# A decoder layer on one core: the first stage takes its operands from a host-transposed copy of the input

## The chip, the core and the metric

The kernel runs on one NeuronCore of a Trainium2 chip. It computes one decoder layer for 1040 rows (16 meta tokens and 1024 tokens) of 1024 channels. The metric is the time on the device of one execution, in microseconds; less is better. The core has five engines that run side by side, each with its own instruction queue in a fixed order: TensorE (PE, matmuls into PSUM), VectorE (DVE), ScalarE (ACT), GpSimd (POOL), and SyncE (SP), which here issues the DMA transfers from HBM. An instruction that waits holds up everything behind it on its engine.

## The reference

The layer is an RMS norm, an input projection, a mix of differential attention (4 heads) and a gated linear recurrence (4 heads), an output projection, and a feed-forward block with a short convolution. The change touches only the norm and the first projections:

```python
def rmsnorm(x, g):
    xf = x.astype(jnp.float32)
    y = xf * lax.rsqrt(jnp.mean(xf * xf, axis=-1, keepdims=True) + EPS)
    return (y * g.astype(jnp.float32)).astype(x.dtype)

h = jnp.concatenate([meta, x], axis=1)          # 1040 rows
a = rmsnorm(h, ln_mix_pre[l])
proj = a @ w_in[l]                              # 1024 x 3584: dq, dk, dv, hq, hf, hi, hg
```

## The kernel before, in words

Every float32 operand of a projection is split into a high part, rounded to the type that PE multiplies at full rate, and a low part, the rest. A projection adds three products: high weight with high operand, low weight with high operand, high weight with low operand. The operand must have channels on the partitions: `ahi` and `alo` hold the normed input transposed, as 8 slices (k = 0 to 7) of 128 channels by 1040 rows.

The rows come in nine blocks (block 0 is the 16 meta rows, blocks 1 to 8 have 128 rows) and in three groups of three blocks: group 0 has 272 columns in the transposed operand, groups 1 and 2 have 384 each. The first stage makes `ahi` and `alo` for all groups and, between, computes dq, dk and dv of attention head 0. For one group and one of the three, that is 24 matmuls: 8 slices times 3 products. All further projections read the same `ahi` and `alo`; the next is `pi_hf`.

Before the change a block goes this way. `load_x` brings its rows. `pre_stat` squares and sums them on ACT and makes 1/rms (two more small ACT instructions). `pre_scale` multiplies the rows on DVE by that factor and by the gain, which is spread over the partitions in `gb` (made by two matmuls `pg` of a column of ones with the gain row). `pre_turn` transposes the 128x128 pieces on PE into PSUM (tile `px`). `pre_hi` casts from PSUM on ACT and `pre_lo` subtracts on DVE. For blocks 4 and 5 `far_block` scales on ACT and POOL.

The order on PE is the order of the program, written by hand (`manual_schedule`). On ACT, DVE and POOL a scheduler places the instructions, except where `state["ordered"]` is set: then they keep the order in which they are written. Before the change this holds for blocks 0 to 5 and group 0; groups 1 and 2 are interleaved by generators. `evac` functions of the attention head (`attn_in`) take a finished projection from PSUM: `ev_q` and `ev_k` write high parts on ACT and low parts (`q`, `kl`) on DVE, `ev_v` copies to `vt`, which `to_nat` (called by `flush`) turns on PE (tile `pn_va`) into `avn`.

Three side jobs lie in the same stretch. `smalls` loads small tables and makes `lb` from `lg`. `lam_terms` makes `nlam` from `lv` by way of `le`. `bias_tables` makes one table per head: it casts a one-hot table to `oh` on ACT, spreads the bias values into `tbb` on DVE, multiplies them on PE (`pb`), copies the result to `rb` on DVE and stores it. Most helpers issue through one wrapper, so the profile names line 58 for them; tiles tell them apart.

## Time and profile before

| | |
|---|---|
| median of 3 runs | 1275.96 us (1275.55 to 1276.72) |
| the profiled execution, first to last instruction | 1275.4 us |
| PE busy | 1256.7 us, 99% of the span |
| DVE, ACT, POOL busy | 913.9, 687.3, 507.2 us |
| mean granted clock of PE | 0.999 |
| HBM read, written | 134.24 MB, 52.17 MB |
| first projection matmul starts | 11.52 us |
| first matmul of pi_hf starts | 57.75 us |

A row of the timeline gives start and duration in us, the engine (PEld is PE's loading of weights, SPq the issue of a DMA), the source line, the operation, the tile written and those read, and how many instructions were merged into the row; in brackets is the idle time before it and what ended it. A row by groups gives after the count the busy time in us and the mean ns of one instruction, and behind the second bar the idle time before such instructions. A row by stretches gives the stretch, its length, the busy time of PE, PEld, DVE, ACT and POOL with counts, then the granted clock, the mean busy share of the DMA engines and the GB/s that they moved.

### The profile page before, as it was taken

The numbers are of one execution on the slowest core, as the hardware profiler recorded it, in microseconds if no ns is written. First come the engines' busy times: TensorE is split into PE (matmuls) and PEld (weight loads), VectorE is DVE, ScalarE is ACT, GpSimd is POOL, SyncE is SP. The second block draws the span as 40 slices with busy tenths as digits, with TensorE's granted clock in tenths as the row PEclk, the third lists the DMA queues.
The fourth block names the chain that finished last, engine by engine and source line by source line (L and its number), as shares of the span: only waits on it lengthen the run. The fifth ranks groups of instructions, "written<-read, shape, count | busy, mean of one in ns | idle before, by whom it ended". The sixth has DMA issues, their size and how long they took to land.

```text
span 1275.4 us, 26064 instructions
## 1 busy us (share of the span) xinstructions
PE 1256.7 (99%) x10166; PEld 1172.8 (92%) x10166; DVE 913.9 (72%) x1492; ACT 687.3 (54%) x1638; POOL 507.2 (40%) x390
## 2 busy tenths in 40 slices
PE   8999999999999999999999999999999999999997
PEld 6999999999999998778899999999999998878886
DVE  7565646565656564457899888898898877797586
ACT  8475456546654754356764544445535445564554
POOL 5232423241323311353067676676776731020121
PEclk9999999999999999999999999999999999999999
DMA  7336555373734533787322221322222247955363
GB/s 260 96 60 131 89 139 94 83 146 92 132 94 79 125 82 113 232 279 253 131 67 67 92 88 63 100 76 75 92 75 83 75 116 258 351 184 173 91 215 124
DMA packets 116705, 165.04 MB, mean 129 GB/s; under 512 B 10131, under 2 KB 57811, under 8 KB 116582
## 3 DMA queue, kind: packets, MB, share of 16 engines
q1 hardware_dynamic: 93350, 151.84, 37.1%
q0 software_dynamic: 23232, 11.54, 7.7%
q8 instruction: 80, 1.31, 0.4%
q14 instruction: 43, 0.35, 0.1%
HBM read 134.24 MB, written 52.17 MB: 146 GB/s over the span
## 4 chain that ended last, share of the span: by engine, by line
PE 46%; DVE 4%; ACT 2%; issue 1%; POOL 1%; DMA 0%; SPq 0%; DVEq 0%; ACTq 0%; POOLq 0%
PE pd L1586 5%; PE pd L1587 5%; PE pd L1585 5%; PE pb L1412 4%; PE pb L1411 4%; PE pb L1413 4%; PE pc L1412 3%; PE pc L1411 3%; PE pc L1413 3%; PE pa L1412 3%; PE pa L1411 3%; PE pa L1413 3%; DVE xh L58 1%; DVE t L58 1%; DVE c L58 1%
## 5 line engine op out<-in xcount | busy, mean ns | idle before, releaser
L1412 PE MATMUL pb<-t,uh 128*128 128x258 f32 x504 | 141.0, 280 | 0.8 <-DVE t L58 0.8
L1411 PE MATMUL pb<-t,uh 128*128 128x258 f32 x504 | 140.5, 279 | 0.8 <-DVE u L58 0.8
L1413 PE MATMUL pb<-t,ul 128*128 128x258 f32 x504 | 140.2, 278 | 0.0
L1586 PE MATMUL pd<-wl,gh 128*128 128x512 f32 (+1 forms) x312 | 121.0, 388 | 1.1 <-DVE wl L58 1.1
L1585 PE MATMUL pd<-wh,gh 128*128 128x512 f32 (+1 forms) x312 | 120.8, 387 | 0.5 <-DVE x L58 0.5
L1587 PE MATMUL pd<-wh,gl 128*128 128x512 f32 (+1 forms) x312 | 120.7, 387 | 0.0
L58 DVE SCALAR_TENSOR_TENSOR c<-uu,cwt,c 128x514 f32<-128x514 f32 (+1 forms) x88 | 106.9, 1214 | 0.0
L58 DVE SCALAR_TENSOR_TENSOR c<-ug,cwt,c 128x514 f32<-128x514 f32 (+1 forms) x88 | 101.4, 1153 | 0.0
L1412 PEld LDWEIGHTS pb<-t,uh 128*128 128x128 f32 x504 | 94.8, 188 | 1.0 <-DVE t L58 1.0
L1411 PEld LDWEIGHTS pb<-t,uh 128*128 128x128 f32 x504 | 94.8, 188 | 1.0 <-DVE u L58 1.0
L58 ACT ACTIVATE c<-c 128x514 f32<-128x514 f32 (+1 forms) x44 | 27.9, 634 | 125.5 <-DVE c L58 125.5
L1413 PEld LDWEIGHTS pb<-t,ul 128*128 128x128 f32 x504 | 94.8, 188 | 0.0
L1412 PE MATMUL pc<-t,uh 128*128 128x258 f32 (+1 forms) x336 | 93.9, 279 | 0.0
L1412 PE MATMUL pa<-t,uh 128*128 128x258 f32 (+1 forms) x336 | 93.9, 279 | 0.0
L1411 PE MATMUL pa<-t,uh 128*128 128x258 f32 (+1 forms) x336 | 93.6, 278 | 0.0
L1411 PE MATMUL pc<-t,uh 128*128 128x258 f32 (+1 forms) x336 | 93.6, 278 | 0.0
L1413 PE MATMUL pc<-t,ul 128*128 128x258 f32 (+1 forms) x336 | 93.4, 278 | 0.0
L1413 PE MATMUL pa<-t,ul 128*128 128x258 f32 (+1 forms) x336 | 93.4, 278 | 0.0
L58 POOL TENSOR_TENSOR ul<-ws,uh 128x512 fp32r<-128x512 f32 x42 | 69.2, 1647 | 59.6 <-ACT uh L58 59.6
L58 POOL TENSOR_TENSOR ws<-ra,ra 128x512 f32<-128x512 f32 x42 | 67.9, 1617 | 60.9 <-DMA ra<-in_wup_dram 34.1
L58 POOL TENSOR_TENSOR c<-c,c 128x514 f32<-128x514 f32 (+1 forms) x44 | 68.8, 1564 | 53.9 <-ACT c L58 50.5
L58 DVE TENSOR_TENSOR ul<-ra,uh 128x512 fp32r<-128x512 f32 x43 | 41.5, 966 | 46.6 <-POOL ul L58 46.6
(389 smaller groups left out, 4183.1 us busy)
## 6 DMA issues: line engine op xcount, KB each, us to landing
ra<-in_wup_dram SPq DMA_DIRECT2D x88, 256.0 KB, 2.6
mp<-msc SPq DMA_DIRECT2D x23, 512.0 KB, 5.7
tsc<-in_wdown_dram SPq DMA_DIRECT2D x44, 256.0 KB, 5.2
wi<-tsc SPq DMA_DIRECT2D x44, 256.0 KB, 3.0
gi<-gsc SPq DMA_DIRECT2D x33, 256.0 KB, 4.2
wi<-in_wdown_dram SPq DMA_DIRECT2D x33, 256.0 KB, 5.2
gsc<-c SPq DMA_DIRECT2D x22, 257.0 KB, 2.1
tsc<-in_wdown_dram POOLq DMA_DIRECT2D x22, 256.0 KB, 7.2
```

The lines of the kernel that those rows point to most:

```text
L58: ins = call(*args, **kw)
L1411: T.matmul(pt, hi[:, s], th[:, k], start=(first and k == 0), stop=False, skip_group_check=True)
L1412: T.matmul(pt, hi[:, s], tl[:, k], start=False, stop=False, skip_group_check=True)
L1413: T.matmul(pt, lo[:, s], th[:, k], start=False, stop=(k == 3), skip_group_check=True)
L1585: T.matmul(py, gh[:, s], wh, start=(k == 0 and pr not in (3, 7)), stop=False, skip_group_check=True)
L1586: T.matmul(py, gh[:, s], wl, start=False, stop=False, skip_group_check=True)
L1587: T.matmul(py, gl[:, s], wh, start=False, stop=(k == NH - 1), skip_group_check=True)
```

## The change

The host now also passes `xt`, a transposed copy of the input (meta rows and x together), laid out by groups. Each group is loaded in two DMAs as channels by rows, into `xr`. The untransposed rows are still loaded, for the sums of squares (`x_stat`: the same three ACT instructions, and a fourth that multiplies the identity by the factor, tile `dg`). `x_spread` multiplies `dg` by a matrix of ones on PE, which puts the factor of every row on all partitions, in PSUM (tile `prs`). `x_norm` multiplies on DVE a slice of `xr` by the gain column and by `prs`; `x_hi` casts a slice to `ahi` on ACT, `x_lo` subtracts for `alo`, on DVE for groups 0 and 2 and on POOL for group 1. The turns on PE and `gb` are gone. The whole first stage is now written out in one order, up to the dq projection of group 2; the same three side jobs stand inside it. Group 1's dq, dk and dv are computed slice by slice together. The number of projection matmuls and their sizes are the same.

```diff
-    def pre_scale(i, half, ss):
-        V.scalar_tensor_tensor(xss[i][:r, cs], xts[i][:r, cs], ss[:r], gb[:r, cs], ALU.mult, ALU.mult)
-    def pre_turn(i, half, pt):
-        for j in range(4):
-            k = 4 * half + j
-            T.transpose(pt[:, j * r:(j + 1) * r], xss[i][:r, P * k: P * (k + 1)], ident[:r, :r])
...
+    def load_xt(g, k0, k1):
+        t0, t1 = span(g)
+        SY.dma_start(xr[g][:, k0:k1], xt[:, KD * t0 + (t1 - t0) * k0:KD * t0 + (t1 - t0) * k1].rearrange("p (k t) -> p k t", k=k1 - k0))
+    def x_stat(i):
         r = rows(i)
         ss = zp.tile([P, 1], F32, tag="ss", name=f"ss{i}", bufs=3)
+        A.activation(x_rows[i][:r], x_rows[i][:r], AF.Square, accum_out=ss[:r])
         rstd_of(ss[:r], ss[:r], D)
+        dg = zp.tile([P, P], F32, tag="dg", name=f"dg{i}", bufs=3)
+        A.mul(dg[:r, :r], ident[:r, :r], ss[:r])
+        return dg
+    def x_spread(g, stats):
+        pt = ps_m(f"prs{g}")
+        o = 0
+        for i in range(*GROUPS[g]):
+            r = rows(i)
+            T.matmul(pt[:, o:o + r], ones[:r], stats[i][:r, :r], start=True, stop=True)
+            o += r
+        return pt[:, :o]
+    def x_norm(g, k, pt):
+        V.scalar_tensor_tensor(xr[g][:, k], xr[g][:, k], gcol[:, k:k + 1], pt, ALU.mult, ALU.mult)
+    def x_hi(g, k):
+        A.copy(ahi[:, k, cols(g)], xr[g][:, k])
+    def x_lo(g, k, eng):
+        return eng.tensor_tensor(alo[:, k, cols(g)], xr[g][:, k], ahi[:, k, cols(g)].bitcast(F32), op=ALU.subtract)
...
+    for i in (1, 2, 0):
+        load_x(i)
+    SY.dma_start(gcol, gpre)
+    for c in range(2):
+        load_xt(0, 4 * c, 4 * c + 4)
+        for j in range(2):
+            load_raw(j, c)
+    for i in (3, 4):
+        load_x(i)
+    for c in range(2):
+        load_raw(2, c)
+    for c in range(2):
+        load_xt(1, 4 * c, 4 * c + 4)
...
+    state["ordered"] = True
+    stats = {i: x_stat(i) for i in (1, 2, 0)}
+    spread = {0: x_spread(0, stats)}
+    for i in (5, 6):
+        load_x(i)
+    for c in range(2):
+        load_xt(2, 4 * c, 4 * c + 4)
...
+    for k in range(KD):
+        x_norm(0, k, spread[0])
+        x_hi(0, k)
+        if k == 5:
+            for j in range(2):
+                w_hi(j, 1, A)
...
+    for k in range(KD):
+        x_lo(0, k, V)
...
+    for i in (3, 4, 5):
+        stats[i] = x_stat(i)
+    for i in (7, 8):
+        load_x(i)
...
+    spread[1] = x_spread(1, stats)
+    for k in range(KD):
+        x_norm(1, k, spread[1])
+        x_hi(1, k)
+        x_lo(1, k, G)
+    for kd in first:
+        kd.out()
...
+    for i in (6, 7, 8):
+        stats[i] = x_stat(i)
+    second = [Kinds(j, 1, ps_m) for j in range(3)]
+    for k in range(KD):
+        for kd in second:
+            kd.mm(k, 0, ahi)
+            kd.mm(k, 1, ahi)
+    flush()
+    smalls()
+    lam_terms()
+    tables = bias_tables()
+    next(tables)
+    for j, kd in enumerate(second):
+        for half in range(2):
+            kd.part(half, 0, alo)
+        if j == 0:
+            spread[2] = x_spread(2, stats)
+    for k in range(KD):
+        x_norm(2, k, spread[2])
+        x_hi(2, k)
+    for kd in second:
+        kd.out()
+    for k in range(KD):
+        last_lo = x_lo(2, k, V)
+    dq = Kinds(0, 2, ps_in)
+    for w, a in ((0, ahi), (1, ahi), (0, alo)):
+        for half in range(2):
+            dq.part(half, w, a)
+    dq.out()
+    flush()
+    state["ordered"] = False
```

How the order on the engines moves is shown at three places. A row is the source line, the operation, the tile written and the tiles read (with buffer numbers), the columns, and how many such rows follow each other.

PE around the first `pb`. Before, it stands behind the last product of group 1:

```order
L252 MATMUL pi_dv_1_506<-ahi,w_246 128x384
L353 MATMUL pb_592<-oh,tbb 128x384
L248 MATMUL pi_dq_2_599<-ahi,wh_dq_0_210 128x384
L250 MATMUL pi_dq_2_599<-alo,wh_dq_0_210 128x384
L252 MATMUL pi_dq_2_599<-ahi,wl_dq_0_211 128x384
```

Now:

```order
L843 MATMUL pi_dv_1_382<-ahi,w_126 128x384 x2
L368 MATMUL pn_va_0_431<-ident,vt_0_358 128x128
L370 MATMUL pn_va_0_431<-ident,vt_0_358 128x128 x2
L354 MATMUL pb_475<-oh,tbb 128x384
L843 MATMUL pi_dq_1_380<-alo,wh_dq_0_154 128x384 x4
L843 MATMUL pi_dq_1_380<-alo,wh_dq_1_158 128x384 x4
L297 MATMUL prs_490<-dg_366,ones 128x128
L297 MATMUL prs_490<-dg_372,ones 128x128
L297 MATMUL prs_490<-dg_378,ones 128x128
L843 MATMUL pi_dk_1_381<-alo,wh_dk_0_156 128x384 x4
```

The first `pb` now stands ahead of the 24 low-operand matmuls of group 1, and the norm factors of group 2 stand behind the first eight of these.

ACT ahead of `oh`. Before, between the squares of blocks 7 and 8 and `oh` (`xs` is a block's scratch, `ss` its sum):

```order
L58 ACTIVATE xs_470,ss_471<-xt_232 128x1024
L58 ACTIVATE ss_428<-ss_428 128x1
L58 ACTIVATE xs_513,ss_514<-xt_304 128x1024
L58 ACTIVATE q_0_120<-pi_dq_1_392 64x384
L58 ACTIVATE q_0_121<-pi_dq_1_392 64x384
L58 CAST ahi<-px_0_434 128x4x128
L58 CAST ahi<-px_1_439 128x4x128
L58 ACTIVATE ss_471<-ss_471,eps 128x1
L58 ACTIVATE ss_514<-ss_514,eps 128x1
L58 ACTIVATE ss_471<-ss_471 128x1
L58 ACTIVATE lg<-lg 128x8
```

Now, from the copy of dv of group 0 (`x_127` and `x_128` are the row buffers, here with blocks 6, 7 and 8):

```order
L58 COPY vt_0_358<-pi_dv_0_247 128x272
L58 ACTIVATE x_127,ss_362<-x_127 128x1024
L58 ACTIVATE dg_366<-ident,ss_362 128x128
L58 ACTIVATE x_128,ss_368<-x_128 128x1024
L58 ACTIVATE dg_372<-ident,ss_368 128x128
L58 ACTIVATE x_128,ss_374<-x_128 128x1024
L58 ACTIVATE dg_378<-ident,ss_374 128x128
L58 COPY avn_122<-pn_va_0_431 16x128
L58 ACTIVATE lg<-lg 128x8
L58 ACTIVATE le<-le 128x2
L58 CAST oh<-ohr 64x384
L58 CAST ahi<-xr_186 128x384 x8
```

(The two one-column rows of each block and the second `avn` copy are left out.) `oh`, `lg` and `le` now stand behind the whole statistics of blocks 6 to 8, which stand behind the evacuation of group 0.

DVE from `nlam` on, now:

```order
L58 TENSOR_SCALAR nlam<-nlam 128x1
L58 CAST tbb<-tb 64x512
L58 TENSOR_TENSOR tbb<-tb,tbb 32x512
L58 COPY rb_477<-pb_475 128x384
L58 TENSOR_SCALAR rb_477<-rb_477 128x256
L58 SCALAR_TENSOR_TENSOR xr_186<-xr_186,gcol,prs_490 128x384 x8
L58 SCALAR_TENSOR_TENSOR q_0_118<-pi_dq_1_380,q_0_118 64x384
L58 SCALAR_TENSOR_TENSOR q_0_119<-pi_dq_1_380,q_0_119 64x384
L58 TENSOR_TENSOR kl_112<-pi_dk_1_381,k_0_120 64x384
L58 TENSOR_TENSOR kl_113<-pi_dk_1_381,k_0_121 64x384
L58 TENSOR_TENSOR alo<-xr_186,ahi 128x384 x8
```

`tbb` stands behind `nlam` (before, ahead of it), and the eight `alo` rows of group 2 stand in one run behind q and kl of group 1; before, the `alo` rows of a block followed its turn.

253 lines of the change are left out of this document (80 added, 173 removed).

## The prediction

> **What bounds the kernel now.** I read the busy shares first, then busy time by stretches, then the instructions of the first 75 us in order of time (PE alone from 42 us on).
>
> ```profile
> PE 1256.7 (99%) x10166; PEld 1172.8 (92%) x10166; DVE 913.9 (72%) x1492; ACT 687.3 (54%) x1638; POOL 507.2 (40%) x390
> 0.00:60.00 60.00, 54.56 (x321) 47.80 (x322) 38.67 (x74) 40.00 (x90) 25.55 (x37) 1.00 0.54 182
> 60.00:160.00 100.00, 99.90 (x1070) 96.32 (x1071) 62.00 (x139) 56.37 (x160) 31.95 (x30) 1.00 0.47 94
> 160.00:260.00 100.00, 99.90 (x824) 97.70 (x823) 55.87 (x129) 60.71 (x185) 29.50 (x26) 1.00 0.51 108
> 11.52 0.78 PE L901 MATMUL pi_dq<-ahi,wh_dq 128*128 128x272 f32 x4
> 42.66 0.44 PE L353 MATMUL pb<-oh,tbb 64*128 64x384 f32 x1
> 57.75 0.28 PE L248 MATMUL pi_hf<-ahi,wh_hf 128*128 128x272 f32 x1
> ```
>
> PE sets the time. It has gaps in the first 60 us and nearly none in the next 200, so whatever the first stage gains or loses goes through to the end. My mark is the first pi_hf matmul, 57.75 us: from there PE's order is the same in both kernels. So the question is only when the changed kernel reaches it. Two more landmarks: the first projection matmul at 11.52, and the first bias table matmul (pb) at 42.66, when 144 of the 216 projection matmuls of head 0 were done.
>
> **What PE is given.** The changed stage has the same 216 projection matmuls, 72 with 272 columns and 144 with 384.
>
> ```profile
> 13.04 0.66 PE L901 MATMUL pi_dq<-ahi,wl_dq 128*128 128x272 f32 x4
> 13.53 0.66 PE L901 MATMUL pi_dq<-alo,wh_dq 128*128 128x272 f32 x4
> 48.21 0.34 PE L248 MATMUL pi_dk<-ahi,wh_dk 128*128 128x384 f32 x1
> 49.77 0.34 PE L248 MATMUL pi_dk<-ahi,wh_dk 128*128 128x384 f32 x1
> 50.41 0.45 PE L250 MATMUL pi_dk<-alo,wh_dk 128*128 128x384 f32 x1
> 50.69 0.34 PE L252 MATMUL pi_dk<-ahi,wl_dk 128*128 128x384 f32 x1
> 38.35 0.97 PEld L287 LDWEIGHTS px<-ident,xs 128*128 128x128 f32 x8
> 71.76 0.39 PE L746 MATMUL pa<-avn,az 128*128 128x128 f32 x2
> 71.98 0.39 PE L746 MATMUL pa<-avn,at 128*128 128x128 f32 x2
> 2.30 3.75 PE L835 MATMUL pg<-grow,ones 1*128 1x512 f32 x4 [2.30 <-DMA grow<-in_gpre_dram]
> ```
>
> From start to start, four 272s take 0.49 us (0.1225 each) and nine 384s 1.56 (0.1735 each): 8.8 + 25.0 = 33.8 us. A pb adds 0.58 (from 49.77 to 50.69 is 0.92, two plain matmuls would be 0.35). Removed: 64 turning transposes of 128 columns at 0.97/8 = 0.12, 7.8 us in all, and the 16-row ones and pg ahead of 11.52. Added: nine norm-factor matmuls of up to 128 columns, 0.22 each (71.98 - 71.76), under 2 us. By PE's work alone the change gains some 6 us. Whether PE can have its operands in time is decided on ACT and DVE.
>
> ```profile
> 18.29 1.08 ACT L58 ACTIVATE xs<-X_in 128x1024 f32<-128x1024 f32 x1
> 20.04 1.15 ACT L58 ACTIVATE xs<-X_in,ss 128x1024 f32<-128x1024 f32 x1
> L58 ACT ACTIVATE on<-po 128x128 f32<-128x128 f32 x36 | 9.5, 273 | 8.2 <-PE po L546 8.2
> L58 ACT CAST k<-k 64x272 fp32r<-64x272 f32 x2 | 0.8, 418 | 0.0
> L58 ACT CAST k<-k 64x384 fp32r<-64x384 f32 x4 | 2.0, 511 | 0.0
> L58 DVE SCALAR_TENSOR_TENSOR q<-pi_dq,q 64x272 fp32r<-64x272 f32 x2 | 0.9, 438 | 0.0
> L58 DVE SCALAR_TENSOR_TENSOR q<-pi_dq,q 64x384 fp32r<-64x384 f32 x4 | 2.2, 556 | 2.4 <-ACT q L58 2.4
> L58 DVE TENSOR_TENSOR wl<-wi,wh 128x512 fp32r<-128x512 f32 x77 | 54.4, 707 | 0.3 <-ACT wh L58 0.3
> L58 DVE TENSOR_TENSOR ul<-ra,uh 128x512 fp32r<-128x512 f32 x43 | 41.5, 966 | 46.6 <-POOL ul L58 46.6
> L58 ACT CAST wh_dq<-wr_dq 128x512 fp32r<-128x512 f32 x2 | 1.3, 630 | 0.0
> L58 POOL TENSOR_TENSOR wl_dq<-wr_dq,wh_dq 128x512 fp32r<-128x512 f32 x2 | 3.0, 1478 | 6.2 <-ACT wh_dq L58 6.2
> 33.29 0.50 ACT L58 CAST oh<-ohr 64x384 fp32r<-64x384 f32 x1
> 27.46 0.41 DVE L58 CAST tbb<-tb 64x512 fp32r<-64x512 f32 x1
> 28.03 0.68 DVE L58 TENSOR_TENSOR tbb<-tb,tbb 32x512 fp32r<-32x512 f32 x1
> ```
>
> Durations taken: one x_stat on ACT 1.9 us (from the square's start to the instruction that uses the factor is 20.04 - 18.29 = 1.75, plus most of a 128x128 scaling, 0.27). x_norm 0.45 for 272 columns and 0.575 for 384: the same operation with a PSUM operand is 0.44 and 0.56, and one follows another a little slower. x_hi 0.44 and 0.53 (casts from SBUF, 0.42 and 0.51). x_lo on DVE 0.53 for 384: three quarters of 0.707; its upper end is three quarters of 0.966. x_lo on POOL 1.05 (from 1.3 to 1.5 for 512). A hand-over between engines about 0.1.
>
> **Loads.** The transposed copy comes beside x, 4.26 MB more ahead of the small tables.
>
> ```profile
> 1.52 0.41 SPq L268 DMA_DIRECT2D xt<-in_x_dram  x1
> 5.28 1.06 ACT L58 ACTIVATE xs<-xt 128x1024 f32<-128x1024 f32 x1 [0.37 <-DMA xt<-in_x_dram]
> 7.00:8.00 1.00, 0.17 (x1) 0.17 (x2) 0.98 (x2) 1.00 (x2) 0.00 (x0) 1.00 0.79 236
> 10.00:15.00 5.00, 4.86 (x36) 4.45 (x35) 3.80 (x9) 4.33 (x11) 4.75 (x5) 1.00 1.04 410
> 20.00:25.00 5.00, 3.91 (x30) 3.29 (x28) 3.53 (x6) 3.83 (x8) 4.12 (x5) 1.00 0.63 196
> ```
>
> The first x block now stands at the head of SP's queue, 0.8 us sooner: it is used from about 4.4. With 0.41 MB per us, and 0.9 us lost in a stretch such as that at 7 us, block 5 (6.95 MB into the queue) lands at 21, block 8 (10.1 MB) at 29, the small tables at 31. None of it is last in the walk below; where block 5 would be, is a rival.
>
> **The walk through the changed order.** Times are us from the start.
> - **Group 0:** three x_stat, 4.4 to 10.0; norm-factor matmuls to 10.5; x_norm and x_hi give the first operand at 11.4. PE starts at 11.5, so its start gains nothing. The two weight casts (0.63 each) between the sixth and the seventh x_hi put the eighth at 15.9. PE then has 56 matmuls left, 6.9 us, to 23.2. The low parts from DVE (17.5) and POOL (19.7) are there before.
> - **Group 1:** meanwhile ACT has two dv casts to 17.2, x_stat 3 to 5 to 23.0. The second norm-factor matmuls end at 23.8; eight x_norm give operands from 25.0, eight x_hi end at 29.2. PE waits 1.4, then does 48 matmuls and the transposes of vt, to 33.9.
> - **First wait.** Next on PE is pb; 24 low-part matmuls stand behind it and do not need it. pb needs oh from ACT and tbb from DVE. ACT has ahead of oh, in order: eight x_hi (29.2), q, k and vt of group 0 (2.85 us, to 32.0), x_stat 6 to 8 (5.7, to 37.7), avn (0.6), lg. DVE has tbb behind lmx, which waits for lg, and behind nlam, which waits for le, which waits for DVE's lv. lg 38.5; five small DVE steps and lv, 1.3; le 0.2; nlam 0.25; tbb 0.41 and 0.68: pb starts at 41.7. PE has waited 7.8 us.
> - **Group 2:** from pb: 0.6; the low part of dq of group 1, 1.4; norm factors of group 2, 44.3; DVE's eight x_norm, 4.6, the last x_hi at 49.7. PE fills 2.8 with dk and dv, then waits 1.2 for the last x_hi; the low-weight part ends at 51.3.
> - **Second wait.** DVE's x_lo of group 2 stand behind q and kl of group 1, and these behind ACT's q and k, which stand behind the eight x_hi: kl ends at 52.5, eight x_lo at 56.75. PE, at 0.1735 a matmul, is fed one each 0.53: done 57.0, 4.3 lost.
> - What is left: vt transposes 0.35, 48 matmuls 8.3, three pb 1.75: the mark at 67.4.
>
> That is **9.7 us after 57.75**. A check by the landmarks: pb comes about when it did (41.7 against 42.66), but with 24 projection matmuls fewer behind it (4.2 us), and the norm factors and the waits after it (0.65 + 1.2 + 4.3) are new: 57.75 - 0.9 + 4.2 + 6.2 is 67.2.
>
> One cost is on top. pg, PE's first work, took 1.87 for 512 columns, against 4 x 0.22 = 0.88 for as many later: half rate, though the clock column reads 1.00. Before, PE had worked since 2.30 when the projections began; now its first work is at 10.0, and there is a wait of 7.8 us in the middle. If each is followed by about as long a stretch at half rate as pg's 3.75 us (by 11.52 the rate was full), the walk gives 70.6, 3.2 more; if neither is, none. The one row of PE after a long rest shows half rate, so I take 2.2 of the 3.2.
>
> [...]
>
> The sum: 9.7 + 2.2 = 11.9 on the profiled 1275.4, 1287.3; the median of the runs lies 0.6 above that execution, so **1287.9**. Low end: no half rate (-2.2), DVE at 0.52 and 0.46 (-1.3), loads 0.5 earlier, and, if ACT never waited, its own work up to oh (31 us from 4.4) puts pb at 37.5, not 41.7; not all at once: 1281.5. High end: all of the half rate (+1.0), DVE beside POOL at 0.65 (+2.2), later loads (+0.8), 1292.
>
> **Rivals.**
> - *Faster: PE's saved work shows.* The place is pb. It decides once ACT and DVE need under 9.9 us from the second norm-factor matmuls to pb (PE's own work in between), where I count 17.4, and feed the low parts as fast. Without both waits and the 1.2 the mark is 67.4 - 13.3 = 54.1, and the time 1272.3. For it: 6 us less PE work. Against it: the ACT order, in which three x_stat alone are 5.7. 6%.
> - *No change: pb's wait alone vanishes*, by a shorter ACT queue: 67.4 - 7.8 = 59.6, 1277.8. 5%.
> - *The loads bind.* If the rate is 0.30 MB/us rather than 0.41 (the row of 20 to 25 us is lower still, though less was asked for there), block 5 lands at 27, 6 later, and spread and all behind it move 5.5: 1293.4. Against it: 410 sustained at 10 to 15. 9%.
> - *Half rate goes on* through the stretches in which PE is fed slowly (the first x_hi, the low parts at one per 0.53) and into the 48 matmuls behind: up to 1.7 us more than the full 3.2: about 1290.6. [...] 14%.
>
> **How the numbers follow.** My forecast, both waits and part of the half rate, 66%: 1287.9. Its range with the fourth rival is 1281.5 to 1292.5. What differs by under 0.2% (2.5 us) counts as no change: faster 6%, same 5%, slower 89%.
>
> **What would show it.** Right: in the changed profile PE's longest wait in the first 60 us is before pb, 6 to 9 us, ended by DVE's tbb or ACT's oh; ACT runs x_stat 6 to 8 in that time; the low parts of dq of group 2 start 0.5 us apart; the mark is at 66 to 71. Wrong: PE reaches the low parts with no wait at pb, or a wait on a DMA is the long one, or the mark is late and the end is not, which would mean slack behind it that I do not see.

## The result, and the profile after

| | before | after |
|---|---|---|
| median | 1276.34 us (1275.55 to 1278.39) | 1296.09 us (1294.22 to 1297.9) |
| the profiled execution, first to last instruction | 1275.4 us | 1293.8 us |
| first projection matmul starts | 11.52 us | 13.41 us |
| first pb starts | 42.66 us | 45.59 us |
| first pi_hf matmul starts (the mark) | 57.75 us | 74.58 us |
| from the mark to the end of the span | 1217.65 us | 1219.2 us |

After over before is 1.0145, with a 95% interval of [1.0127, 1.0164]. The change makes the kernel slower, by 19.75 us between the medians. The forecast, 1287.9 us, has the direction and about 60% of the size; the time lies 3.6 us above the range. The kernels of the experiments with the changed first stage leave 1.9 to 2.1 us outside their span, as the changed kernel does (2.0); before and e14 leave 1.8.

The 19.75 divide so: 16.83 lie ahead of the mark; 1.55 behind it in the two profiled executions (it is shown below that this part varies by as much without any change there); 0.2 outside the span; and 1.15 is the choice of the executions that were profiled (by what lies outside the span, that of before took about 1277.2, 0.9 above its median; that of after 1295.81, 0.3 below). So the experiments ask about the mark.

The same views as before, of the changed kernel. First the busy shares, and busy time by stretches (PE, PEld, DVE, ACT, POOL, then the granted clock).

```profile
PE 1256.9 (97%) x10108; PEld 1174.3 (91%) x10108; DVE 910.2 (70%) x1496; ACT 692.1 (53%) x1653; POOL 511.8 (40%) x394
...
0.00:60.00 60.00, 36.93 (x185) 33.25 (x185) 26.20 (x64) 39.18 (x93) 22.53 (x32) 0.94 0.59 215
60.00:160.00 100.00, 99.91 (x827) 95.31 (x827) 57.27 (x130) 55.15 (x156) 28.62 (x27) 0.97 0.43 101
```

PE's busy time over the whole span is as before (1256.9 against 1256.7), although it has the turns no longer to do. In the first 60 us it is busy for 36.9 us where it was 54.6, and then, in the next 100, it again has hardly a gap. Two numbers are new: the clock is 0.94 and 0.97 in these stretches. A busy PE is there a slow PE, which is how the saved work is hidden in the first row.

The timeline of PE (start, duration), at the steps that the prediction names. The long wait in the middle is the one before pb, 7.57 us. No wait on a transfer is among PE's in the first 75 us.

```profile
10.55 1.73 PE L297 MATMUL prs<-dg,ones 16*128 16x16 f32 x6 [10.55 <-ACT dg L58]
13.41 0.57 PE L843 MATMUL pi_dq<-ahi,wh_dq 128*128 128x272 f32 x1 [1.13 <-ACT ahi L58]
...
18.16 1.11 PE L843 MATMUL pi_dq<-ahi,wl_dq 128*128 128x272 f32 x4
19.06 1.11 PE L843 MATMUL pi_dk<-ahi,wl_dk 128*128 128x272 f32 x4
...
22.00 1.16 PE L843 MATMUL pi_dv<-ahi,w 128*128 128x272 f32 x8
23.00 1.15 PE L843 MATMUL pi_dq<-alo,wh_dq 128*128 128x272 f32 x8
...
26.98 0.83 PE L297 MATMUL prs<-dg,ones 128*128 128x128 f32 x6
29.06 0.44 PE L843 MATMUL pi_dq<-ahi,wh_dq 128*128 128x384 f32 x1 [1.25 <-ACT ahi L58]
...
45.59 0.65 PE L354 MATMUL pb<-oh,tbb 64*128 64x384 f32 x1 [7.57 <-DVE tbb L58]
46.18 2.93 PE L843 MATMUL pi_dq<-alo,wh_dq 128*128 128x384 f32 x8
48.90 1.02 PE L297 MATMUL prs<-dg,ones 128*128 128x128 f32 x6
49.68 1.64 PE L843 MATMUL pi_dk<-alo,wh_dk 128*128 128x384 f32 x8
...
58.62 3.97 PE L843 MATMUL pi_dq<-alo,wh_dq 128*128 128x384 f32 x8 [1.94 <-DVE alo L58]
...
64.26 0.52 PE L250 MATMUL pi_dk<-alo,wh_dk 128*128 128x384 f32 x1
...
74.58 0.29 PE L248 MATMUL pi_hf<-ahi,wh_hf 128*128 128x272 f32 x1
```

Compare like with like. Four matmuls of 272 columns are 0.91 apart at 18.16, 0.49 in the kernel before. Eight of 384 take 2.93 at 46.18 and 1.64 at 49.68. One of 384 columns takes 0.52 at 64.26 and 0.34 from 66.44 on. These are three separate stretches of work at half rate: the first ends at about 22.0 (eight matmuls of 272 columns then take 1.00 from start to start), the second runs from pb at 45.6 to about 49.3 and the third from about 59.5 to 66.3. The stretches of 5 us show the second and the third in the clock, which is the first number behind the five busy times (an average of 0.57 over 5 us is half rate for 4.3 of them, one of 0.95 for the last 0.5):

```profile
45.00:50.00 5.00, 4.41 (x17) 4.11 (x18) 1.42 (x4) 0.00 (x0) 0.20 (x1) 0.57 0.12 41
...
55.00:60.00 5.00, 3.00 (x12) 2.02 (x12) 4.21 (x9) 3.02 (x7) 0.00 (x0) 0.95 0.00 0
60.00:65.00 5.00, 5.00 (x14) 3.51 (x14) 2.88 (x6) 2.59 (x5) 1.93 (x3) 0.50 0.14 50
65.00:70.00 5.00, 5.00 (x25) 4.57 (x24) 1.72 (x5) 0.76 (x2) 2.28 (x2) 0.86 0.29 98
```

The first stretch doesn't show there: the clock column reads 1.00 in this execution until its first fall, at 42.46 (0.96 from 42.0 to 42.5), although matmuls of 272 columns are 0.227 us apart from 13.78 on. Durations, not the column, tell the rate at the start here.

### The profile page after: what moved, and what is told of

It is laid out like the page before. It is cut to its first block, busy times and chain, and to the rows that moved or that the text cites. A ratio compares the mean times of both kernels' runs of the same rounds, so it can differ in the third digit from the quotient of the medians.

```text
span 1293.8 us, 25973 instructions
## 1 busy us (share of the span) xinstructions
PE 1256.9 (97%) x10108; PEld 1174.3 (91%) x10108; DVE 910.2 (70%) x1496; ACT 692.1 (53%) x1653; POOL 511.8 (40%) x394
## 3 DMA queue, kind: packets, MB, share of 16 engines
q8 instruction: 79, 1.29, 0.4%
## 4 chain that ended last, share of the span: by engine, by line
PE 45%; DVE 5%; ACT 2%; issue 1%; DMA 0%; SPq 0%; DVEq 0%; ACTq 0%
PE pd L1562 5%; PE pd L1563 4%; PE pd L1561 4%; PE pb L1388 4%; PE pb L1387 4%; PE pb L1389 4%; PE pc L1388 3%; PE pc L1387 3%; PE pc L1389 3%; PE pa L1388 3%; PE pa L1387 3%; PE pa L1389 3%; DVE xh L58 1%; DVE t L58 1%; ACT a L58 1%
## 5 line engine op out<-in xcount | busy, mean ns | idle before, releaser
L58 POOL TENSOR_TENSOR ws<-ra,ra 128x512 f32<-128x512 f32 x42 | 67.4, 1604 | 61.5 <-DVE c L58 31.3
L58 POOL TENSOR_TENSOR c<-c,c 128x514 f32<-128x514 f32 (+1 forms) x44 | 69.0, 1567 | 54.9 <-ACT c L58 49.9
```

Source lines behind the costliest of these rows:

```text
L58: ins = call(*args, **kw)
```

## The experiments

The theory to be tested, A where an expectation uses letters: the waits are those of the prediction's walk, and what the mark is late beyond it is PE at half rate after each rest. Its rivals: the operands come late for another reason (DVE and POOL in each other's way, loads), or something behind the mark takes its share. "warm" in the edits below is a burst of matmuls of 128 columns, ones by identity, whose result nobody reads; no other engine has work from it. A ratio is against runs of before on the same chip.

| kernel | mark, us | median, us | over before [95%] | mark to end, us |
|---|---|---|---|---|
| before | 57.75 | 1276.34 | | 1217.65 |
| after | 74.58 | 1296.09 | 1.0145 [1.0127, 1.0164] | 1219.2 |
| e1_fill_pb | 73.04 | 1292.87 | 1.0118 [1.0091, 1.0144] | 1217.6 |
| e2_fill_start | 74.33 | 1293.78 | 1.0127 [1.0105, 1.0150] | 1217.8 |
| e3_fill_all | 69.97 | 1292.42 | 1.0114 [1.0091, 1.0136] | 1221.4 |
| e9_dense_start | 74.92 | 1295.55 | 1.0141 [1.0125, 1.0156] | 1218.1 |
| e4_tables_later | 66.95 | 1296.96 | 1.0149 [1.0128, 1.0171] | 1228.5 |
| e5_low_early | 68.92 | 1290.44 | 1.0103 [1.0088, 1.0118] | 1220.4 |
| e6_tables_early | 70.64 | 1290.5 | 1.0101 [1.0085, 1.0118] | 1218.7 |
| e7_both | 63.49 | 1284.27 | 1.0058 [1.0040, 1.0077] | 1217.5 |
| e8_best | 62.72 | 1290.19 | 1.0105 [1.0090, 1.0120] | 1225.5 |
| e10_best2 | 65.96 | 1287.53 | 1.0081 [1.0065, 1.0098] | 1220.1 |
| e11_best3 | 57.27 | 1278.88 | 1.0014 [1.0005, 1.0024] | 1219.6 |
| e12_best3_nofill | 56.72 | 1278.6 | 1.0013 [1.0002, 1.0024] | 1218.3 |
| e13_best4 | 54.40 | 1276.86 | 1.000 [0.999, 1.001] | 1221.4 |
| e14_before_input | 57.72 | 1277.51 | 1.0008 [0.9998, 1.0018] | 1217.3 |

The mark and the last column are of the one profiled execution. The kernels e1, e2 and e9 have after's order behind the mark; their last column is 1217.6 to 1218.1, after's is 1219.2, before's 1217.65. A difference of 1.5 there is no effect of the change that these runs could show. The marks scatter too: behind the same wait at pb, half rate lasted to 49.3 in after and to 50.6 in e9, which has the same order there. And the intervals of e1 to e4 reach about 3 us to either side, so that the medians of e1, e2 and e3 don't tell these three apart; the prices of single stretches below are read from one profiled execution each.

### Filling PE's rests

**e1: PE kept busy through the wait before pb.**

```diff
     flush()
+    warm(28, "warm1")
     smalls()
```

> The changed kernel with 28 matmuls of ones by the identity (128 columns, about 0.22 us each) put on PE ahead of the first pb, into a bank that nobody reads: they fill some 6.2 of the 7.57 us wait, and no wait of the program is taken away. Theory A (half rate after each rest is what the prediction sized too small): pb still starts at about 45.6, but pb, the low parts of dq and the norm factors of group 2 behind it run at full rate (0.44 + 1.5 + 0.65 in place of 0.65 + 2.93 + 1.02), the mark moves from 74.58 to about 72.7, the time from 1296.1 to about 1294.2. Rival B (these matmuls are slow because their operands or PSUM are contended for, not because PE rested): the pitch of the low parts stays near 0.34, the mark and the time stay within 0.5 us.

```profile
37.61 6.42 PE L304 MATMUL warm<-ident,ones 128*128 128x128 f32 x56
45.35 0.41 PE L360 MATMUL pb<-oh,tbb 64*128 64x384 f32 x1 [1.32 <-DVE tbb L58]
45.69 1.66 PE L849 MATMUL pi_dq<-alo,wh_dq 128*128 128x384 f32 x8
```

The eight low-part matmuls after pb take 1.66 instead of 2.93, and pb itself still starts when tbb is ready (45.35). The mark comes 1.54 earlier. So the half rate after pb is caused by PE's rest and not by its operands, and it is worth about 1.5 us in this execution's mark.

**e2: PE kept busy from 1.6 us on, until the first factors come.**

```diff
+    warm(26, "warm0")
     state["ordered"] = True
     stats = {i: x_stat(i) for i in (1, 2, 0)}
```

> The changed kernel with 26 such matmuls at the head of PE's order, ending before the first norm factors (by about 9.5 us). Theory A: the norm factors of group 0 take 0.9 rather than 1.73, the projections start near 12.6 rather than 13.41 and run at 0.124 a matmul from the start, group 0 ends at about 23.4 rather than 26.98, and everything behind it, pb included, comes 3.6 earlier: mark 71.0, time about 1292.5. Rival B: group 0 still takes until 26 or later; time within 0.5 us of 1296.1. A rival in between: PE's gain in group 0 is lost before pb, because ACT (statistics, casts, evacuation) has no slack there: group 0 ends 3.6 earlier, pb less than 1 earlier.

The expectation missed: the mark moves by 0.25 where 3.6 were expected, and group 0 still runs at half rate. The stretches of 1 us, around the end of the burst and around the return:

```profile
11.00:12.00 1.00, 0.72 (x5) 0.52 (x4) 0.24 (x1) 0.00 (x0) 1.00 (x1) 0.78 1.08 422
...
21.00:22.00 1.00, 1.00 (x7) 1.00 (x7) 0.00 (x0) 0.62 (x3) 1.00 (x2) 0.60 1.04 414
...
42.00:43.00 1.00, 0.00 (x0) 0.00 (x0) 0.90 (x7) 0.00 (x0) 0.00 (x0) 0.64 0.00 0
...
49.00:50.00 1.00, 1.00 (x9) 1.00 (x9) 0.33 (x1) 0.00 (x0) 0.00 (x0) 0.95 0.01 3
```

The clock falls at 11.56 (an average of 0.78 is full rate for 0.56 of that us) although PE has had only two short rests, 1.53 before the factors and 1.13 before the first operand. It comes back only at 21.8. Filling one rest was not enough here, where the work behind it comes in pieces.

**e3: both bursts, and one such matmul between each two low-part matmuls of group 2.**

```diff
+    pw = warm(8, "warm2")
+    for k in range(KD):
+        if k:
+            T.matmul(pw[:, :P], ones, ident, start=True, stop=True)
+        dq.mm(k, 0, alo)
```

> All three rests filled: the start, the wait at pb, and the slowly fed low parts of group 2 (8 matmuls of ones by the identity in the wait before them and one between each two). Theory A: no stretch at half rate is left; the mark comes where the prediction's walk at full rate has it, 67 to 68, the time is about 1288.7; what it gains beyond the sum of the other two fillings (about 5.5) is the third half-rate stretch, about 1.8. Rival B: the third stretch stays slow, the gain is at most the sum of the other two.

```profile
44.62 0.41 PE L360 MATMUL pb<-oh,tbb 64*128 64x384 f32 x1 [1.31 <-DVE tbb L58]
...
55.99 0.44 PE L849 MATMUL pi_dq<-alo,wh_dq 128*128 128x384 f32 x1 [0.15 <-DVE alo L58]
...
59.27 0.44 PE L849 MATMUL pi_dq<-alo,wh_dq 128*128 128x384 f32 x1
...
60.80 0.34 PE L252 MATMUL pi_dk<-ahi,wl_dk 128*128 128x384 f32 x1
```

The mark is 4.6 earlier than after's. The low parts still arrive 0.47 apart (55.99 to 59.27 for eight), but the matmuls behind them now take 0.34 and not 0.52. The landmarks divide the 4.6: pb starts 0.97 earlier than in after (group 0 ends earlier, though it still runs at half rate from 13.3 to 20.1), the first low part of group 2 starts 2.63 earlier (55.99 against 58.62), the mark 4.61. So 1.0 lies in group 0, 1.7 is the second stretch and 2.0 the third, the one that begins while PE is fed by DVE. In after the third runs from 62.4, when the feeding is over, to 66.3 at half rate, which costs the same 2.0. Rival B is out by the mark; but the mark was expected at 67 to 68, and the time gained only 3.7: the part behind the mark was 2.2 longer in the profiled execution, in which PE rested 2.0 us before a `py` matmul and the mean clock of the 100 us from 469.97 on was 0.98; after has no such rest there, and 1.00 in the same stretch.

**e9: the start with no rest left.** Fillers until the first operand and then between all pairs of group 0's high parts.

```diff
+    warm(28, "warm0")
...
+    for k in range(KD):
+        for _ in range(6 if k == 0 else 4 if k == 4 else 1):
+            T.matmul(pw[:, :P], ones, ident, start=True, stop=True)
+        for kd in (dq, dk):
+            kd.mm(k, 0, ahi)
```

> The changed kernel with PE kept busy without a hole from 1.6 us on: 28 matmuls of ones by the identity ahead of the norm factors of group 0, 6 between these and the first projection, one per slice between the first 16 projections and 4 in the hole that the two weight casts make. Filling only up to 9.1 us had left group 0 at half rate until 21. Theory A1 (the clock falls when PE was less than about half busy for some 3 us, whether in one rest or in pieces, and needs 4 to 5.5 us of nearly unbroken work to return): no half rate now, group 0 ends at 23.4 rather than 26.98, and pb, with all that follows, comes 3.6 earlier: mark about 71.0, time about 1292.5. Rival B1 (group 0 is slow for another cause, such as the 412 GB/s of loads beside it or DVE and ACT on the same memory): the pitch of its matmuls stays at 0.227 and group 0 ends at 26 or later, mark within 0.7 of 74.6.

```profile
17.54 0.66 PE L849 MATMUL pi_dq<-ahi,wl_dq 128*128 128x272 f32 x4
19.16 0.76 PE L849 MATMUL pi_dq<-ahi,wl_dq 128*128 128x272 f32 x4 [0.47 <-POOL wl_dq L58]
20.40 0.77 PE L849 MATMUL pi_dk<-ahi,wl_dk 128*128 128x272 f32 x4 [0.47 <-POOL wl_dk L58]
...
25.98 0.83 PE L297 MATMUL prs<-dg,ones 128*128 128x128 f32 x6
```

Now group 0 has the full rate (0.49 for four, 17.54 to 18.03) beside the same loads, so the pitch that rival B1 gives is out; but it ends at 25.98, where 23.4 was expected: 1.0 earlier than in after, and 2.8 later than the walk's 23.2. PE meets a wait that half rate had covered, the second half of the low weights from POOL. What POOL did there stands in the changed kernel's timeline:

```profile
10.65 1.27 POOL L58 TENSOR_TENSOR wl_dq<-wr_dq,wh_dq 128x512 fp32r<-128x512 f32 x1
...
15.59 2.90 DVE L58 TENSOR_TENSOR alo<-xr,ahi 128x272 fp32r<-128x272 f32 x8
...
15.91 3.72 POOL L58 TENSOR_TENSOR wl_dq<-wr_dq,wh_dq 128x512 fp32r<-128x512 f32 x1 [2.77 <-ACT wh_dq L58]
```

The same subtraction takes 1.27 and once 3.72, and the long one begins 0.3 us after DVE's run of eight x_lo and outlasts it by 1.1. e8 (below) has this subtraction ahead of x_lo, beside x_norm:

```profile
13.48 1.29 POOL L58 TENSOR_TENSOR wl_dq<-wr_dq,wh_dq 128x512 fp32r<-128x512 f32 x1
```

And in e11, where POOL began first (13.95 against 14.22), its subtractions beside x_lo take 1.30 and 1.49, and the eight x_lo take 4.88, in after 2.90. In e8 x_lo began first (18.37), and still POOL's subtraction of dv's weights from 18.53 took 1.42 and the eight x_lo 3.99. So the longer times stand where the two overlap, on POOL in after and mostly on DVE in e8 and e11; what decides between them, these rows don't show. The mark didn't gain from e9: in that execution the second and the third stretch at half rate lasted to 50.6 and 67.7, where after's lasted to 49.3 and 66.3.

### Taking the waits away

**e4: the tables and all that leads to pb written behind the last x_lo of group 2.**

```diff
     flush()
-    smalls()
-    lam_terms()
-    tables = bias_tables()
-    next(tables)
...
+    smalls()
+    lam_terms()
+    tables = bias_tables()
+    next(tables)
     dq.out()
     flush()
     state["ordered"] = False
```

> The side jobs (small tables, lambda terms, bias tables) are written behind the x_lo of group 2, and the four pb stand between the dv matmuls of group 2. Theory A (pb's place in the order makes the wait): PE goes from group 1 straight into its low parts at about 38, waits some 2.2 us for the last statistics at the norm factors of group 2 (41.7), never waits at pb; last x_hi at 47.3; the wait for x_lo of about 2 us and the half rate behind it stay. Mark about 67.9, time about 1289.4. Rival C (ACT and DVE work, or the 4.26 MB more of loads, sets the pace, so that the wait only moves): PE waits at the norm factors or at pb as long as before, 6 us or more in all beyond what it waits for x_lo, and the time stays above 1294.

```profile
75.14 0.38 PE L665 MATMUL S<-k,q 128*128 128x16 f32 x1 [6.18 <-DVE rb L58]
```

(The four tables are also spread otherwise between the matmuls of group 2.) The mark is 7.6 earlier, by as much as the wait at pb, and about where it was expected, but the time is not better at all (1296.96), as rival C had it. The wait came back 8 us behind the mark, before the first score matmul S, which was released by DVE's rb. rb is one buffer: each table's copy waits for the store of the one before (DVE's copy at 71.51 waited 3.43 for it), and four tables now follow each other closely. Pushing a chain back moves its wait.

**e6: the same chain moved forward instead**, ahead of x_stat 7 and 8; pb stays where it was.

```diff
-    for i in (6, 7, 8):
+    smalls()
+    stats[6] = x_stat(6)
+    lam_terms()
+    tables = bias_tables()
+    next(tables)
+    for i in (7, 8):
         stats[i] = x_stat(i)
...
     flush()
-    smalls()
-    lam_terms()
-    tables = bias_tables()
     next(tables)
```

> The changed kernel with ACT's and DVE's part of the side jobs written ahead of the statistics of blocks 6 to 8 (of 6, the lambda terms; of 7 and 8, the rest); PE's order is not changed. Moving the tables behind group 2 took pb's wait away and moved the mark by 7.6 us, but turned it into a wait at the first scores. Theory A (pb waits for the place of oh and tbb behind 6.2 us of statistics): oh and tbb are done at about 39, pb waits 1 to 1.5 us; the norm factors of group 2 then wait for the last statistics, until about 42.6; x_norm of group 2 starts at 43.3 rather than 49.96, the wait for x_lo and the half rate behind it stay; mark 67.9, no wait at the first scores, time about 1289.4. Rival C (the wait only moves to the norm factors): these wait until 46 or later, and the time stays above 1293.

The timeline of PE, and then two stretches of PE alone (busy time, clock, share of the DMA engines, GB/s):

```profile
41.33 0.41 PE L355 MATMUL pb<-oh,tbb 64*128 64x384 f32 x1 [2.97 <-ACT x L58]
```

```profile
39.60:43.00 3.40, 1.67 (x9) 1.00 0.00 0
43.00:46.40 3.40, 3.40 (x13) 0.50 0.66 213
```

The wait at pb shrinks from 7.57 to 2.97; more than expected is left. The row puts its end down to an ACT square that was over at 41.10, but DVE's tbb ended later, at 41.18: from lg (37.41) the chain of small steps on DVE and ACT, with x_stat 6 within it, still takes 3.8 us. PE works again from 41.33, and the clock still falls, at 43.0, for 3.4 us: PE had been busy for 1.67 of the 3.4 us before. The mark comes at 70.64, the time is 5.6 below after's.

**e5: half of group 2's x_lo moved to POOL beside x_norm, the others ahead of q and kl on DVE.**

```diff
     for k in range(KD):
         x_norm(2, k, spread[2])
         x_hi(2, k)
+        if k < 4:
+            x_lo(2, k, G)
+    for k in range(4, KD):
+        x_lo(2, k, V)
     for kd in second:
         kd.out()
-    for k in range(KD):
-        last_lo = x_lo(2, k, V)
```

> The changed kernel with the x_lo of group 2 taken from behind q and kl of group 1: slices 0 to 3 on POOL as soon as their x_hi is done, 4 to 7 on DVE right behind the x_norm. Theory A (this place in the order makes the second wait, and the slow feeding of PE there makes the third half-rate stretch): the first wait stays at 7.6; PE goes through the low-operand part of dq of group 2 with no wait over 0.5, ending at about 58 rather than 62.4, and dk of group 2 starts at 0.1735 a matmul at once: mark about 68.5, time about 1290.0. Rival (the half rate there has nothing to do with the feeding): the wait goes, the half rate stays, mark about 70.3, time 1291.8. Rival (q and kl, now late, hold up PE): a new wait of 2 us or more at the turns of vt or at the first scores.

```profile
56.77 1.70 PE L843 MATMUL pi_dq<-alo,wh_dq 128*128 128x384 f32 x8
```

The second wait is gone: the eight low-part matmuls go in 1.70 instead of 3.97, without the 1.94 before them, and the third half-rate stretch goes with them (the mark is 5.66 earlier: 1.94 of wait, 2.3 of slow feeding, the rest half rate behind). The expectation holds within 0.5 us.

**e7: e5 and e6 together.**

> The two moves together: x_lo of group 2 split between POOL and DVE ahead of q and kl (alone it moved the mark from 74.58 to 68.92), and the side jobs ahead of the statistics of blocks 6 to 8 (alone: 70.64). Theory A (two separate waits, each with its own half-rate stretch behind it): the moves add, the mark comes at 64.5 to 65.5, the time at about 1285. Rival (one wait stands in for the other, since ACT and DVE are the bound): the mark stays at 67 or later, the time at 1288 or more.

The mark is at 63.49 and the time at 1284.27, 11.8 us below after. e5 gave 5.7 and e6 5.6 alone: the two waits are separate and add up (the mark comes 1.0 ahead of the expected 64.5 to 65.5). This is 60% of what the change cost, and two moves in the order give it.

### How far the changed stage can be mended

**e8: everything at once.** Beside e5, the three statistics of a group share one rsqrt and `dg` is made on DVE; the chain to pb stands behind group 1's casts, ahead of x_stat 6 to 8; the small loads that pb needs come first; fillers at the start.

```diff
+    def x_stats(g, blocks):
+        ss = zp.tile([P, 3], F32, tag="ss", name=f"ss{g}", bufs=3)
...
+            A.activation(x_rows[i][:r], x_rows[i][:r], AF.Square, accum_out=ss[:r, c:c + 1])
+        rstd_of(ss, ss, D)
...
+            V.tensor_scalar(dg[:r, :r], ident[:r, :r], ss[:r, c:c + 1], None, ALU.mult)
```

> All of it together: PE filled ahead of group 0 and its first slices given four matmuls each (high and low weights); the three sums of squares of a group share one Ln and one Exp, and dg is made on DVE; the casts of the second weight halves stand ahead of the x_hi; the norm factors of a group stand ahead of the last low-operand part of the group before; small loads and side jobs ahead of the statistics of group 2; x_lo of group 2 half on POOL; dq, dk and dv of group 2 slice by slice together. The same arithmetic, with 30 matmuls that nobody reads more. Theory A (order, statistics' length and half rate account for all of the loss): PE starts at about 12.5, has no wait over 1.5 us before the mark, which is at 51.5 to 53.5, earlier than the 57.75 of before; time 1272 to 1275, under the kernel before. Rival D (three norm passes on DVE and three casts on ACT bound the stage, whatever the order): the mark stays at 57 or later and the time at or above that of the kernel before.

```profile
12.45 0.62 ACT L58 CAST wh_dq<-wr_dq 128x512 fp32r<-128x512 f32 x1 [3.72 <-DMA wr_dq<-in_win_dram]
14.21 0.37 PE L857 MATMUL pi_dq<-ahi,wh_dq 128*128 128x272 f32 x1 [2.20 <-ACT ahi L58]
22.29 1.06 ACT L58 ACTIVATE x<-x 128x1024 f32<-128x1024 f32 x1 [3.89 <-DMA x<-in_x_dram]
...
37.46 0.56 PE L368 MATMUL pb<-oh,tbb 64*128 64x384 f32 x1 [2.11 <-DVE tbb L58]
37.96 2.93 PE L857 MATMUL pi_dq<-alo,wh_dq 128*128 128x384 f32 x8
```

Ten us behind what was expected, and here the prediction's rival of the loads appears: with ACT faster, it waits 3.72 for a weight and 3.89 for block 5. A rest of 2.11 at pb is again followed by half rate (2.93); the one of 2.20 before 14.21 is not (four matmuls of 272 columns then take 0.49 from start to start). The stretch around that one, PE alone (busy time, clock, share of the DMA engines, GB/s):

```profile
10.25:13.67 3.42, 1.76 (x14) 1.00 1.04 415
```

Behind the mark, at the first S, PE waits 3.5 us for DVE's kl.

**e10: e8 with the loads in another order and the chain to pb split** (lg, le and nlam behind group 2's x_lo, the tables' casts ahead of x_stat 6 to 8), and the other moves that its expectation lists. Block 5 was loaded earlier, and the load was written ahead of block 1's square, in whose buffer it lands; so in this kernel the sum of squares of block 1 is taken over block 5's rows, and the first square waits for them.

```diff
-    for i in (3, 4):
+    for i in (3, 4, 5):
         load_x(i)
     for c in range(2):
         load_raw(2, c)
```

> The combined kernel of before, mended where its trace showed new waits. There ACT stood 3.72 us for the second halves of the dq and dk weights and 3.89 us for block 5, both ended by a DMA, the small tables held up tbb until 37.3, and q and kl of group 2 came too late for the first scores (3.5 us). Now block 5 is loaded ahead of the dv weights and the transposed group 1, the weight casts stand behind the fourth x_hi, tbb and oh no longer stand behind the lambda and lb terms, which go behind x_lo of group 2, and dq and dk of group 2 are taken out before dv is finished. Theory A (order and half rate account for the loss): PE starts at about 12.2, runs group 0 to about 23, group 1 to 31, has no rest over 1.5 us and no half rate, mark at 50.5 to 54, no wait at the first scores, time 1270 to 1274, 0.2 to 0.5% under the kernel before. Rival E (with the order mended the loads bind: 4.26 MB more at 0.41 MB a us): ACT or DVE waits of 2 us and more for block 5, for the transposed group 1 or for blocks 7 and 8 remain, PE rests there and falls to half rate, mark at 56 or later, time at or above the kernel before.

The first square starts at 16.93 (4.17 in after), so the times say nothing on what was to be tested, except that a start 12.8 us later costs only part of it: the mark is at 65.96. What follows is the next kernel.

**e11: e10 with the loads of block 5, of dv's weights and of group 1's `xr` written behind x_stat 1, 2, 0.**

```diff
     x_stats(0, (1, 2, 0))
     spread = {0: x_spread(0, stats)}
-    load_x(6)
+    load_x(5)
+    for c in range(2):
+        load_raw(2, c)
+    for c in range(2):
+        load_xt(1, 4 * c, 4 * c + 4)
+    load_x(6)
```

> The combined kernel with the load of block 5 written behind the statistics of block 1, whose buffer it takes; before, it stood ahead of them, so that the first square waited for block 5 until 16.93 (and summed the wrong block), PE started 10.6 us late, and the mark still came at 65.96. From the norm factors on (21.51) that run took 44.5 us to the mark. Theory A: the norm factors come at about 10.1 again, PE is warm there, so that group 0 loses no half rate (about 2.5 in that run): mark at 51.5 to 54, time 1272 to 1275. Rival E (loads bind): block 5, the transposed group 1 or block 8 land late, ACT or DVE wait for a DMA for 2 us or more, PE rests: mark 55 to 57, time 1276 to 1278, no better than the kernel before.

```profile
31.33 0.51 ACT L58 CAST oh<-ohr 64x384 fp32r<-64x384 f32 x1 [3.44 <-DMA ohr<-in_onehot_dram]
31.52 1.17 DVE L58 CAST tbb<-tb 64x512 fp32r<-64x512 f32 x1 [4.18 <-DMA tb<-in_table_dram]
...
36.74 1.31 PE L302 MATMUL prs<-dg,ones 128*128 128x128 f32 x6 [1.96 <-DVE dg L58]
37.70 2.91 PE L853 MATMUL pi_dk<-alo,wh_dk 128*128 128x384 f32 x8
```

The mark is level with before (57.27), the time 0.14% above it, as rival E had it. The small tables now arrive late; ACT and DVE wait for them. A rest of 1.96 is followed by 2.91 for eight matmuls.

**e12: e11 without its fillers.**

```diff
-    warm(26, "warm0")
...
-    pw = warm(4, "warm1")
```

> The same without the 30 matmuls that nobody reads. In the changed kernel filling gained 1.0 us in group 0, because POOL's low weights of the second halves then came last (19.2 and 20.4). Here the weight casts stand earlier. Theory A1: without filling, the norm factors take 1.7 rather than 1.0 and group 0 runs at half rate for 5 us or more; mark 2.5 to 3.5 later than with it. Rival (something else, loads or POOL, ends group 0 anyway): within 1 us of it.

```profile
15.62 0.43 PE L853 MATMUL pi_dq<-ahi,wl_dq 128*128 128x272 f32 x1
```

The time doesn't change measurably: mark 56.72, ratio 1.0013. Half rate came back as Theory A1 has it (norm factors 1.72 against 1.03, matmuls of 272 columns 0.227 apart from 13.1 to 17.0), but it costs almost nothing: group 1 starts at 25.12, in e11 at 24.85. At full rate PE waits in e11 for POOL's low weights (0.41 and 0.72) and is fed the low parts of dq in 1.82 for eight; at half rate they are there before (1.15). Here half rate is hidden where the operands hold PE up anyway.

**e13: e11 with x_stat 6 to 8 ahead of the tables' casts, `dg` of group 1 back on ACT.**

```diff
+    x_stats(2, (6, 7, 8))
+    dq.out()
     tables = bias_tables()
     next(tables)
-    dq.out()
-    x_stats(2, (6, 7, 8))
```

> The combined kernel with one more change of order: the statistics of blocks 6 to 8 ahead of oh and tbb on ACT and DVE (there ACT stood 3.44 us and DVE 4.18 us for the small tables' DMAs, the norm factors of group 2 waited 1.96 and the clock fell to half for the 8 matmuls behind), and dg of group 1 made on ACT, which was idle there. Theory A: the wait at the norm factors of group 2 goes, and with it some 2.2 us of half rate, and 0.7 at group 1: mark 52 to 53, time 1273 to 1275, faster than the kernel before by 0.1 to 0.3%. Rival E (loads bind): the wait comes back at another place that a DMA ends (tables at pb, blocks 7 and 8 at their squares); mark 55 or later, time 1276.5 or more.

Here the mark is 3.35 *earlier* than before's (52 to 53 was expected), no half rate is left behind the first fillers, and the time is the same: 1.000 [0.999, 1.001]. The reason lies behind the mark. The sums of stretches that make 1200 us behind the mark (busy time of each engine, then the means), first of before and then of e13:

```profile
sum 1200.00, PE 1193.84 PEld 1118.38 DVE 864.91 ACT 640.30 POOL 478.72; mean PE 79.59 PEld 74.56 DVE 57.66 ACT 42.69 POOL 31.91
```

```profile
sum 1200.00, PE 1191.50 PEld 1116.73 DVE 866.63 ACT 640.33 POOL 482.35; mean PE 79.43 PEld 74.45 DVE 57.78 ACT 42.69 POOL 32.16
```

PE idles 2.3 us more there, of the 3.7 us by which that part is longer. Single waits in it, far from the first stage, come and go between executions of kernels that have the same order there (1.7 us before an `ss` matmul in after, none in e1), so these profiles don't say which of them an earlier mark causes. In e13 the two largest that before does not have are one before an output projection matmul and one of 1.6 before a `pd` matmul, ended by DVE's wl (0.4 at most in before):

```profile
517.19 0.39 PE L1038 MATMUL py<-woh,mp 128*128 128x512 f32 x1 [1.63 <-issue]
```

Why they are there stays open.

**e14: before, with the extra input passed and 16 columns of it loaded.**

```diff
     load_x(8)
+    xd = zp.tile([P, 16], F32, tag="xd", name="xd", bufs=1)
+    SY.dma_start(xd, xt[:, :16])
```

> The kernel before with the host-transposed copy as one more input, of which one DMA of 16 columns is loaded and nothing used. All kernels with the copy take about 2 us more from the mark to the end than the kernel before (1218 to 1220 against 1217). Theory F (the further input, by where it puts the others in memory or by what lies outside the span, costs these 2 us): the time is 1.5 to 2.5 us over the kernel before. Rival: the 2 us come from the changed first stage (what it leaves to DVE, POOL and the DMA queues) or are the scatter of single executions; the time is within 0.7 us of the kernel before.

1.0008 [0.9998, 1.0018], with the mark unmoved at 57.72: about 1 us, and between -0.3 and 2.3, so it can't be told from nothing, nor from the 1.5 of Theory F. The profiled execution speaks against the theory: 1217.3 from the mark to the end and 1.8 outside the span, as in before. Whether the input by itself takes a part of e13's 3.35 us is not settled; all of it, it does not.

## Why the prediction was wrong, step by step

| step | predicted, us | measured, us |
|---|---|---|
| first x is used | 4.4 | 4.17 |
| one x_stat | 1.9 | 2.04 |
| norm-factor matmuls of group 0 | 0.5 | 1.73 |
| PE's first projection | 11.5 | 13.41 |
| group 0 done | 23.2 | 26.98 |
| first operand of group 1 | 25.0 | 29.06 |
| x_stat 6 to 8 end | 37.7 | 41.60 |
| pb, and the wait before it | 41.7, 7.8 | 45.59, 7.57 |
| norm factors of group 2 | 44.3 | 49.9 |
| last x_hi | 49.7 | 54.8 |
| last x_lo; each apart | 56.75; 0.53 | 61.85; 0.48 |
| mark | 69.65 (67.4 and 2.2) | 74.58 |

**What was right.** The direction and its cause. PE's saved work doesn't count; ACT's order decides, with x_stat 6 to 8 ahead of what pb needs, and then DVE's order, with q and kl ahead of x_lo. Both waits were found with their place and size from the trace of before (7.57 against 7.8; low parts 0.47 apart against 0.53, and 4.3 us lost there, as predicted: 62.39 - 56.68, less 1.4 of work), and e5, e6 and e7 show that removing them gives 5.7 and 5.6 us, separately. From the first operand of group 1 to pb the walk was 16.7 long and took 16.5.

**The step that failed: the 2.2 us taken for half rate.** The text said "I take 2.2 of the 3.2", two stretches of about 3.75 us. The measured price is 4.6 (e3), over three stretches: 1.0 in group 0 (e9, all at full rate there, gains the same 1.0), 1.7 behind pb and 2.0 from the low parts of group 2 on. The two that were foreseen cost 2.7, only 0.5 more than was taken. The second worked at half rate for about as long as pg's row suggested (3.7), the first for some 8.6 us, in which PE was handed group 0's high parts in pieces; most of its price was hidden, because POOL's low weights would have held up a faster PE (e9). The third, 2.0, stands at nothing in the sum, and that is the term that failed. It is the rival "half rate goes on", which had 14%; its mechanism, its place and nearly its size (1.7) were right, and e5 and e3 each remove it. Low parts that come one per 0.53, with 0.17 of work each, were in the walk; that the clock falls under such feeding, no row of before showed.

**The second step: "are there before" for POOL's low weights.** Group 0 ended 3.8 us later than in the walk. At full rate (e9) it is still 2.8 later than the walk has it, from two things: the first operand comes 1.9 later than 11.5 (1.4 in e9; in after, 0.4 is x_stat and 1.2 the norm-factor matmuls), and POOL's subtraction of 3.72 us beside x_lo, where the prediction's row shows a mean of 1.48 (in e9 it makes the two waits before 19.16 and 20.40, 1.4 in all). The walk behind it stands on these times, so 2.6 of the 7.2 us between the full-rate mark of 67.4 and the measured one is left when the 4.6 are taken off.

**Two small ones.** The profiled execution of before was set 0.6 below the median of the runs; by what lies outside the span it was about 0.9 above. And 1.55 us behind the mark were not foreseen; the runs show that this part varies by as much, and its cause is not settled. So the 8.2 us between forecast and measurement are 2.4 of half rate (4.6 - 2.2), 2.6 from group 0, 1.55 behind the mark, and 1.7 outside the spans and in which executions were profiled. (A slip without weight: from the second norm factors to pb the walk's own times give 17.9, 41.7 - 23.8, where the first rival says 17.4.)

**What would have shown it.** Apart from PE's start, the longest wait in the first 60 us is before pb, ended by tbb, in the 6 to 9 us given; ACT runs x_stat 6 to 8 in it; the low parts come half a us apart. The mark, given as 66 to 71, was 74.58. No transfer holds PE in the changed kernel, so the rival of the loads did not come about there; it did as soon as ACT was relieved (e8, e11), which is where it belongs: the second limit behind the first. Even there the place in the orders counts as much as the rate: e13 has the loads of e11, and its mark is 2.9 earlier by moves on ACT and DVE alone.

## What to carry to other kernels

Work that is taken off the engine that bounds a kernel is gained only if its operands can follow: walk the other engines' orders up to the first place where the bound engine waits, and look for what stands ahead of it there by order alone. On PE, add up its work over some 3.4 us: where that was less than half here, by a rest (1.67 of 3.40 busy in e6) or by a rest and slow feeding (1.54 of 3.5 in after), a second payment followed, 3 to 9 us of work at half rate (3.4 in e6, some 8.6 in after's group 0). In e12 it cost almost nothing, since the operands held PE up anyway. And move a chain that feeds a wait forward rather than back (e6 gained, e4 only moved the wait), one wait at a time, since the next limit, here the loads, shows only then.
